# Log-sum-exp over rows: moving the early logarithm forward and redrawing the table of chunks

## Chip, cores, metric

One core of a Trainium2 chip. The metric is the device time of the kernel in microseconds (us), as a median of several executions. The profile is one execution; its "span" runs from the first to the last instruction and is some 1.8 us shorter than the time. All runs quoted here are on record as undisturbed ("fast"), with a granted clock of 1.0. TensorE does nothing in this kernel. "DVE" is VectorE, "ACT" is ScalarE, "SPq" is the queue of SyncE, which issues the loads.

## The reference

```python
x = np.random.randn(32, 512, 1024).astype(np.float32)   # 64 MiB (67.1 MB)
x_max = np.max(x, axis=-1, keepdims=True)
out = x_max.squeeze(-1) + np.log(np.sum(np.exp(x - x_max), axis=-1))
```

With normal inputs the kernels take log(sum(exp(x))) without the maximum, and both pass the comparison with the reference.

## The kernel before

The 16,384 rows lie as 128 rows on each of 128 partitions. "A row" below means one such row on all 128 partitions: 128 x 1024 numbers, 512 KB. The rows are loaded in 18 chunks into a ring of 51 row slots. A pair `(rows, n_dve)` in the table says how many rows a chunk has and how many of them take the first of two ways:

- *bulk rows*: one Exp of ScalarE over all `n_dve` rows, then one sum of VectorE;
- *accumulator rows*: one Exp of ScalarE per row, which sums along the row as it goes; a short accumulator read follows.

```python
CHUNKS = [
    (4, 0), (16, 10), (14, 13), (15, 4), (16, 7), (15, 6), (12, 9), (9, 6), (7, 5), (5, 4),
    (4, 3), (3, 3), (2, 2), (2, 0), (1, 1), (1, 0), (1, 0), (1, 0),
]
RING_ROWS = 51
LN_EARLY = 6
# ... cut: tensors, semaphores, place[i] = (ring slot, first row) ...
    def take_logs(lo, hi, dve_wait, act_wait):
        nonlocal acts
        nc.scalar.wait_ge(act_done, act_wait)
        nc.scalar.wait_ge(dve_done, dve_wait)
        nc.scalar.activation(out=res[:, lo:hi], in_=sums[:, lo:hi], func=Ln).then_inc(
            act_done, 1
        )
        acts += 1
# ... cut ...
    for i, (r, n_dve) in enumerate(CHUNKS):
        if i:
            load(i)              # SyncE waits until the ring slots are free, then issues
        s, row = place[i]
        if i == len(CHUNKS) - LN_EARLY:
            logged = place[i - 1][1]
            take_logs(0, logged, *done_before[i - 1])
        nc.scalar.wait_ge(landed[i], 16)
        if n_dve:
            nc.scalar.activation(
                out=ring[:, s : s + n_dve], in_=ring[:, s : s + n_dve], func=Exp
            ).then_inc(act_done, 1)
            acts += 1
            nc.vector.wait_ge(act_done, acts)
            nc.vector.reduce_sum(
                out=sums[:, row : row + n_dve], in_=ring[:, s : s + n_dve], axis=AX
            ).then_inc(dve_done, 1)
            # ... cut ...
        for j in range(n_dve, r):
            nc.scalar.activation(
                out=ring[:, s + j],
                in_=ring[:, s + j],
                func=Exp,
                accum_out=sums[:, row + j : row + j + 1],
            ).then_inc(act_done, 1)
            # ... cut ...
    take_logs(logged, NB, dves, acts)
    nc.scalar.wait_ge(act_done, acts)
    nc.scalar.dma_start(out=out_v, in_=res).then_inc(stored, 16)
```

So one Ln over the first 117 columns of sums stands before chunk 12, and the other 11 columns are done at the end.

Of the kernel before, what the change touches and what calls it, by code (L numbers as in the profile page):

```python
# [1 line left out]

# [4 lines left out]



CHUNKS = [  # L10
    (4, 0), (16, 10), (14, 13), (15, 4), (16, 7), (15, 6), (12, 9), (9, 6), (7, 5), (5, 4),
    (4, 3), (3, 3), (2, 2), (2, 0), (1, 1), (1, 0), (1, 0), (1, 0),
]
RING_ROWS = 51

LN_EARLY = 6


@with_exitstack
def kernel(  # L20
    ctx: ExitStack,
    tc: tile.TileContext,
    x: bass.AP,
    axis: bass.AP,
    out: bass.AP,
):
    nc = tc.nc
    P = nc.NUM_PARTITIONS

    assert axis in (-1, len(x.shape) - 1), f"only last-axis reduction supported, got {axis}"  # L30

    x_flat = x.flatten_outer_dims()
    N, D = x_flat.shape
    assert N % P == 0
    NB = N // P
    assert sum(r for r, _ in CHUNKS) == NB

    fp32 = mybir.dt.float32
    Exp = mybir.ActivationFunctionType.Exp
    Ln = mybir.ActivationFunctionType.Ln  # L40
    AX = mybir.AxisListType.X

    x_v = x_flat.rearrange("(p t) d -> p t d", p=P)
    out_v = bass.AP(tensor=out.tensor, offset=out.offset, ap=[[NB, P], [1, NB]])

    ring = nc.alloc_sbuf_tensor("ring", [P, RING_ROWS, D], fp32).ap()
    sums = nc.alloc_sbuf_tensor("sums", [P, NB], fp32).ap()
    res = nc.alloc_sbuf_tensor("res", [P, NB], fp32).ap()

    landed = [tc.alloc_semaphore(f"landed{i}") for i in range(len(CHUNKS))]  # L50
    act_done = tc.alloc_semaphore("act_done")
    dve_done = tc.alloc_semaphore("dve_done")
    stored = tc.alloc_semaphore("stored")


    hook = nc.pop_inst_callback()
    symbolic, nc._always_lower_symbolic_ap = nc._always_lower_symbolic_ap, False


    place = []  # L60
    row = slot = 0
    for r, _ in CHUNKS:
        if slot + r > RING_ROWS:
            slot = 0
        place.append((slot, row))
        slot += r
        row += r



    busy = [(0, 0)] * RING_ROWS
    acts = dves = 0

    def load(i):
        (s, row), r = place[i], CHUNKS[i][0]
        act_wait = max(a for a, _ in busy[s : s + r])
        dve_wait = max(d for _, d in busy[s : s + r])
        if dve_wait:
            nc.sync.wait_ge(dve_done, dve_wait)
        if act_wait:  # L80
            nc.sync.wait_ge(act_done, act_wait)
        nc.sync.dma_start(out=ring[:, s : s + r], in_=x_v[:, row : row + r]).then_inc(  # L82
            landed[i], 16
        )

    def take_logs(lo, hi, dve_wait, act_wait):
        nonlocal acts
# [7 lines that stand above are left out]
    body = nc.main_func.blocks[-1]  # L95
    assert not body.instructions
    load(0)
    n_early = len(body.instructions)

    nc.scalar.preload_act_table_set("natural_log_exp_and_others")  # L100

    logged = 0
    done_before = [(0, 0)]
    for i, (r, n_dve) in enumerate(CHUNKS):
        if i:
            load(i)
        s, row = place[i]
        if i == len(CHUNKS) - LN_EARLY:
            logged = place[i - 1][1]
            take_logs(0, logged, *done_before[i - 1])  # L110
        nc.scalar.wait_ge(landed[i], 16)
        if n_dve:
            nc.scalar.activation(  # L113
                out=ring[:, s : s + n_dve], in_=ring[:, s : s + n_dve], func=Exp
# [6 lines that stand above are left out]
            dves += 1  # L121
            for j in range(n_dve):
                busy[s + j] = (0, dves)
# [8 lines that stand above are left out]
            busy[s + j] = (acts, 0)  # L132
        done_before.append((dves, acts))
# [4 lines that stand above are left out]
    nc.gpsimd.wait_ge(stored, 16)  # L138



    sp = mybir.EngineType.SP
    first = nc.main_func.blocks[0]
    head, work = first.instructions, body.instructions
    at = next(k for k, i in enumerate(head) if i.engine == sp and i.opcode == "Drain")
    end = next(k for k, i in enumerate(head) if i.opcode == "UnconditionalBranch")
    first.instructions = head[:at] + work[:n_early] + head[at:end] + work[n_early:] + head[end:]
    body.instructions = []

    nc._always_lower_symbolic_ap = symbolic  # L150
    nc.push_inst_callback(hook)


# [1 line left out]
_INS = ['x', 'axis']  # L155
_OUTS = [((32, 512), 'float32')]

_NUMBERS = {'axis': -1}


# [26 lines left out]
```

## Time and profile before

| | before |
|---|---|
| time, median of the first 3 runs | 164.24 us (164.04 to 164.56) |
| span of the profiled run | 162.7 us |
| load queue, busy share of 16 DMA engines | 96.1% |
| ScalarE / VectorE busy | 76% / 49% |
| final Ln starts | 159.94 us |

The page's queue line of the kernel before: packets, MB moved, share of the span of all 16 DMA engines.

```profile
q1 hardware_dynamic: 2592, 67.11, 96.1%
```

96.1% of 162.7 us is 156.3 us: the loads fill the program but for its first microsecond and its end. As long as the packets take as long as they do here, nothing that only rearranges work on the engines can go below that.

The waits view of the same profile: engine, line, operand, what it waited for; total us, number of waits, the longest.

```profile
DVE sums L118 <- ACT ring L113: 79.0, 5, 35.6
ACT ring L113 <- DMA ring<-in_x_dram: 30.2, 5, 15.0
ACT ring L125 <- DMA ring<-in_x_dram: 5.5, 1, 5.5
...
ACT res L90 <- DVE sums L118: 0.4, 1, 0.4
```

ScalarE waits for loads six times, the last time before chunk 5 at 99.85 us. After that its only recorded wait is 0.4 us before the early Ln (L90), for VectorE's sums.

The timeline of its end: start, duration, engine, line, operation. L125 is an accumulator row, L90 the Ln.

```profile
151.67 0.30 ACT L90 ACTIVATE res<-sums 128x117 f32<-128x117 f32 x1 [0.41 <-DVE sums L118]
...
157.74 1.04 ACT L125 ACTIVATE ring<-ring 128x1024 f32<-128x1024 f32 x1
...
158.78 1.04 ACT L125 ACTIVATE ring<-ring 128x1024 f32<-128x1024 f32 x1
159.72 0.18 ACT L125 ACTIVATION_READ_ACCUMULATOR ring<-ring 128x1 f32 x1
159.94 0.21 ACT L90 ACTIVATE res<-sums 128x11 f32<-128x11 f32 x1
```

### The profile page before, as it was taken

What the parts mean: (1) busy time and instruction counts of PE and PEld (TensorE: products, weight loads), DVE (VectorE), ACT (ScalarE), POOL (GpSimd) and SP (SyncE); (2) the same over time, 40 slices, a digit from 0 to 9 for tenths busy, and PEclk for the clock granted to TensorE, in tenths of its full rate; (3) what the DMA queues carried; (4) which work ended last, traced back from release to release, by engine and by line L of the source; (5) the groups of instructions that cost most, each with busy time, mean ns of one, the idle gap of its engine ahead of it and who ended that gap; (6) DMA issues with size and microseconds to landing.
All of it is one profiled execution on the core that took longest, in us unless ns stands there. A gap on an engine that the chain in (4) does not pass through costs nothing.

```text
span 162.7 us, 208 instructions
## 1 busy us (share of the span) xinstructions
DVE 79.2 (49%) x13; ACT 123.2 (76%) x126; POOL 0.2 (0%) x4
## 2 busy tenths in 40 slices
DVE  0000000029940499990003940194009999999980
ACT  3180004999599707999099984999999999999893
POOL 0000000000000000000000000000000000000000
DMA  7997999989999979989997998998999999999960
GB/s 262 511 515 306 467 515 437 409 352 409 439 483 483 468 321 451 515 354 421 499 468 332 408 483 387 435 507 362 426 435 415 430 423 432 420 420 422 405 268 16
DMA packets 2737, 67.18 MB, mean 413 GB/s; under 512 B 304, under 2 KB 432, under 8 KB 944
## 3 DMA queue, kind: packets, MB, share of 16 engines
q1 hardware_dynamic: 2592, 67.11, 96.1%
q10 hardware_dynamic: 144, 0.07, 0.1%
q14 instruction: 1, 0.01, 0.0%
HBM read 67.11 MB, written 0.07 MB: 413 GB/s over the span
## 4 chain that ended last, share of the span: by engine, by line
DMA 45%; DVE 27%; ACT 26%; issue 0%; SPq 0%; ACTq 0%
DMA ring<-in_x_dram 45%; DVE sums L118 27%; ACT ring L113 17%; ACT ring L125 9%; ACT res L90 0%; SPq L82 0%; ACTq L89 0%
## 5 line engine op out<-in xcount | busy, mean ns | idle before, releaser
L118 DVE TENSOR_REDUCE sums<-ring 128x4 f32<-128x4096 f32 (+9 forms) x13 | 79.2, 6138 | 79.0 <-ACT ring L113 79.0
L113 ACT ACTIVATE ring<-ring 128x4096 f32<-128x4096 f32 (+9 forms) x13 | 64.8, 4987 | 30.3 <-DMA ring<-in_x_dram 30.2
L125 ACT ACTIVATE ring<-ring 128x1024 f32<-128x1024 f32 x55 | 57.2, 1040 | 5.5 <-DMA ring<-in_x_dram 5.5
L125 ACT ACTIVATION_READ_ACCUMULATOR ring<-ring 128x1 f32 x55 | 10.3, 187 | 0.0
L100 ACT ACT_TABLE_LOAD x1 | 1.3, 1283 | 0.8 <-PEq L168 0.8
L90 ACT ACTIVATE res<-sums 128x117 f32<-128x117 f32 (+1 forms) x2 | 0.5, 256 | 0.4 <-DVE sums L118 0.4
L168 POOL MEMSET const-bfloat16-1.0<- 128x1 bf16 x1 | 0.1, 102 | 0.0
L168 POOL MEMSET const-uint8-127<- 128x1 uint8 x1 | 0.1, 102 | 0.0
L168 POOL MEMSET const-float32-0.0<- 128x1 f32 x1 | 0.1, 99 | 0.2 <-issue 0.2
L168 POOL MEMSET const-float32-1.0<- 128x1 f32 x1 | 0.1, 99 | 0.0
## 6 DMA issues: line engine op xcount, KB each, us to landing
ring<-in_x_dram SPq DMA_DIRECT2D x2, 7680.0 KB, 45.3
ring<-in_x_dram SPq DMA_DIRECT2D x1, 7168.0 KB, 42.6
ring<-in_x_dram SPq DMA_DIRECT2D x1, 6144.0 KB, 40.9
ring<-in_x_dram SPq DMA_DIRECT2D x1, 4608.0 KB, 29.7
ring<-in_x_dram SPq DMA_DIRECT2D x2, 2048.0 KB, 20.0
ring<-in_x_dram SPq DMA_DIRECT2D x1, 3584.0 KB, 36.5
ring<-in_x_dram SPq DMA_DIRECT2D x1, 2560.0 KB, 28.1
ring<-in_x_dram SPq DMA_DIRECT2D x2, 1024.0 KB, 29.4
```

Source lines behind the costliest of these rows:

```text
L90: nc.scalar.activation(out=res[:, lo:hi], in_=sums[:, lo:hi], func=Ln).then_inc(act_done, 1)
L100: nc.scalar.preload_act_table_set("natural_log_exp_and_others")
L113: nc.scalar.activation(out=ring[:, s : s + n_dve], in_=ring[:, s : s + n_dve], func=Exp).then_inc(act_done, 1)
L118: nc.vector.reduce_sum(out=sums[:, row : row + n_dve], in_=ring[:, s : s + n_dve], axis=AX).then_inc(dve_done, 1)
L125: nc.scalar.activation(out=ring[:, s + j], in_=ring[:, s + j], func=Exp, accum_out=sums[:, row + j : row + j + 1],).then_inc(act_done, 1)
L168: nc = _bacc.Bacc("TRN2", target_bir_lowering=False, num_devices=1)
```

## The change

Its intent: keep the early Ln from interrupting ScalarE near the end, by putting it in front of chunk 5, and draw the chunks so that the shares of ScalarE and VectorE fit the moments at which the chunks land. The new list for the first load, FIRST_PARTS, is set to one load as before; the placement code at the end was made general. Neither is meant to change what runs.

```diff
 CHUNKS = [
-    (4, 0), (16, 10), (14, 13), (15, 4), (16, 7), (15, 6), (12, 9), (9, 6), (7, 5), (5, 4),
-    (4, 3), (3, 3), (2, 2), (2, 0), (1, 1), (1, 0), (1, 0), (1, 0),
+    (4, 1), (15, 11), (16, 10), (16, 15), (16, 0), (14, 0), (12, 9), (9, 5), (7, 5), (5, 4),
+    (4, 3), (3, 0), (2, 2), (2, 2), (1, 0), (1, 0), (1, 0),
 ]
-LN_EARLY = 6
+LN_AT = 5
+FIRST_PARTS = [("sync", 0, 128)]
@@ in the loop over chunks
-        if i == len(CHUNKS) - LN_EARLY:
-            logged = place[i - 1][1]
-            take_logs(0, logged, *done_before[i - 1])
-        nc.scalar.wait_ge(landed[i], 16)
+        if i == LN_AT:
+            logged = row
+            take_logs(0, logged, *done_before[i])
+        nc.scalar.wait_ge(landed[i], 16 * (len(FIRST_PARTS) if i == 0 else 1))
```

(Cut: the loop over FIRST_PARTS in `load`, and the placement of the first load.)

More of the change, by code (lines that the diff above doesn't have):

```diff
@@ L81, in load @@
             nc.sync.wait_ge(act_done, act_wait)
-        nc.sync.dma_start(out=ring[:, s : s + r], in_=x_v[:, row : row + r]).then_inc(
-            landed[i], 16
-        )
+        for engine, lo, hi in FIRST_PARTS if i == 0 else [("sync", 0, P)]:
+            getattr(nc, engine).dma_start(
+                out=ring[lo:hi, s : s + r], in_=x_v[lo:hi, row : row + r]
+            ).then_inc(landed[i], 16)
     def take_logs(lo, hi, dve_wait, act_wait):
@@ L138 @@
     nc.gpsimd.wait_ge(stored, 16)
-    sp = mybir.EngineType.SP
     first = nc.main_func.blocks[0]
     head, work = first.instructions, body.instructions
-    at = next(k for k, i in enumerate(head) if i.engine == sp and i.opcode == "Drain")
     end = next(k for k, i in enumerate(head) if i.opcode == "UnconditionalBranch")
-    first.instructions = head[:at] + work[:n_early] + head[at:end] + work[n_early:] + head[end:]
+    head, tail = head[:end], head[end:]
+    for ins in work[:n_early]:
+        at = next(
+            k for k, i in enumerate(head) if i.engine == ins.engine and i.opcode == "Drain"
+        )
+        head.insert(at, ins)
+    first.instructions = head + work[n_early:] + tail
     body.instructions = []
```

## The prediction

> **What bounds the kernel now.** The loads. The queue table gives the load queue 96.1% of 16 engines' span (156.3 of 162.7 us). By windows of one microsecond, data flows from 1.2 until about 157.3 us, with no lasting hole: 67.11 MB / 156.1 us = 430 GB/s. The Trainium skill ("DMA: Bandwidth & Descriptors", Specifications) puts the fabric ceiling at 435 GB/s; the trace is about 1% below, so reordering chunks can hardly shorten this part.
>
> Then comes a tail. In the timeline ScalarE is busy from 99.85 us (landing of row 80) to 159.9, except 0.41 us before the first Ln, where it waits for VectorE's sums (waits view). The final Ln starts at 159.94, the span ends at 162.7. The last row lands at about 157.5 at the latest and costs 1.04 us plus an accumulator read, so the final Ln could start at about 158.7 at best. What can be removed is 1.2 us, 0.7%. The 45% DMA of the chain of waits understates the loads: the chain follows the backlogged engines.
>
> **What the change does**, with the trace's durations (bulk Exp 0.107 + 0.853 us per row as pitch, row with accumulator 1.04, VectorE sum 0.13 + 1.07 per row, rows landing every 1.21 us):
> - The early Ln leaves the saturated stretch: 0.41 wait + 0.30 work. It moves to about 101 us, the edge of ScalarE's last idle gap. Exp and Ln share a table set (Trainium skill, "ScalarE: Activation LUTs", Table sets; the trace has one table load of 1.28 us), so moving it adds no load.
> - ScalarE's work after chunk 5 lands: before, 39 bulk rows in 9 instructions plus 24 accumulator rows = 59.2 us from 99.85. After, 30 bulk rows in 7 plus 31 accumulator rows = 58.6 us, but chunk 5 ends one row later, landing at about 101.0. Chunk 4 (16 accumulator rows, 16.6 us from about 84.1) ends at 100.8, then Ln until about 101.0. The last Exp ends at about 159.7.
> - VectorE ends its last sum at 159.3 to 159.5 instead of 158.2: nearly a tie with ScalarE.
> - The final Ln takes 61 columns instead of 11: +0.04 us.
> - One load fewer: 128 of 2592 packets. In a stream without holes, nothing visible.
> - The first four chunks fill the ring exactly (51 rows). Chunk 4's load can issue at about 47 us (VectorE done with chunk 1) while queued data last until 64; chunk 7's at about 94 with data until 115. No hole.
> - The rewritten placement leaves the first load where it was.
>
> **Sum:** on the critical path 0.7 us leaves with Ln and 0.6 us of work, 1.15 us of later landing comes in: the final Ln moves by about -0.2 us (estimate, +-0.6). Predicted 164.0 us, 163.3 to 164.7. Chances: faster by over 2% 0.01, within 2% 0.98, slower 0.01.
>
> **What the profile would show.** Right: load queue again about 156 us busy, data ending at 157 to 158; Ln at about 101 with little wait before it; ScalarE unbroken from 101 to about 159.6; last VectorE sum within 1 us of the last Exp; final Ln at 159.2 to 160.2. Wrong: a hole in the load stream after 20 us, an idle gap of ScalarE over 0.5 us after 101, or Ln waiting for VectorE.
>
> **What would make it wrong.** A load queue that runs dry at a ring wait, since chunks 4 and 5 keep all rows on ScalarE; a stream whose rate changes by 1% with chunk sizes (1.6 us, more than all the rest); or VectorE, with two 2-row sums at the end, finishing over 1 us after ScalarE.

## The result, and the profile after

The changed kernel took 164.12 us (median of 6 runs, 163.90 to 164.65), the kernel before 164.28 us (6 runs). The ratio of the fast runs is 0.9994, with a 95% interval of 0.9974 to 1.0015. Ratios here are the mean time of one kernel's fast runs over that of the other's in the same rounds, so they are not quite the ratio of the medians. In a second comparison (run `a_again` below) the ratio was 0.9982 (0.9965 to 0.9999). The change is worth at most about 0.3%, and the first comparison alone does not tell it from nothing; the 0.2 us predicted lie in both intervals.

The page's queue line of the changed kernel, and its waits view:

```profile
q1 hardware_dynamic: 2448, 67.11, 96.4%
```

```profile
DVE sums L121 <- ACT ring L116: 85.9, 7, 29.6
ACT ring L116 <- DMA ring<-in_x_dram: 29.4, 4, 14.0
ACT ring L128 <- DMA ring<-in_x_dram: 5.3, 1, 5.3
...
```

96.4% of 162.2 us is again 156.4 us of loading. The wait of the Ln for VectorE is gone. The timeline of the changed kernel, at the new place of the Ln and at the end:

```profile
99.29 1.04 ACT L128 ACTIVATE ring<-ring 128x1024 f32<-128x1024 f32 x1
...
100.46 0.26 ACT L93 ACTIVATE res<-sums 128x67 f32<-128x67 f32 x1
100.67 1.06 ACT L128 ACTIVATE ring<-ring 128x1024 f32<-128x1024 f32 x1
...
157.15 1.04 ACT L128 ACTIVATE ring<-ring 128x1024 f32<-128x1024 f32 x1
...
158.19 1.04 ACT L128 ACTIVATE ring<-ring 128x1024 f32<-128x1024 f32 x1
159.14 0.19 ACT L128 ACTIVATION_READ_ACCUMULATOR ring<-ring 128x1 f32 x1
159.36 0.25 ACT L93 ACTIVATE res<-sums 128x61 f32<-128x61 f32 x1
```

The final Ln starts 0.58 us earlier than in the profile before, 159.36 instead of 159.94. The medians moved by only 0.16 us. The six times of the changed kernel range over 0.75 us, and its profiled execution (163.96 us) is one of its faster ones, while that of before (164.53 us) is one of its slower ones. **One pair of profiles exaggerates the difference here**; 0.43 us of the 0.58 us is another course of the load stream and not the change, as the table under b_half and a_again shows.

### The profile page after: what moved, and what is told of

Same layout as the page of the kernel before. It is cut to its first block, busy times and chain, and to the rows that moved or that the text cites. A ratio compares the mean times of both kernels' runs of the same rounds, so it can differ in the third digit from the quotient of the medians.

```text
span 162.2 us, 213 instructions
## 1 busy us (share of the span) xinstructions
DVE 72.9 (45%) x11; ACT 124.1 (76%) x136; POOL 0.2 (0%) x4
## 3 DMA queue, kind: packets, MB, share of 16 engines
q1 hardware_dynamic: 2448, 67.11, 96.4%
HBM read 67.11 MB, written 0.07 MB: 414 GB/s over the span
## 4 chain that ended last, share of the span: by engine, by line
ACT 52%; DMA 38%; DVE 7%; issue 1%
DMA ring<-in_x_dram 38%; ACT ring L128 30%; ACT ring L116 22%; DVE sums L121 7%; ACT res L93 0%
## 5 line engine op out<-in xcount | busy, mean ns | idle before, releaser
L121 DVE TENSOR_REDUCE sums<-ring 128x5 f32<-128x5120 f32 (+8 forms) x11 | 72.9, 6648 | 86.0 <-ACT ring L116 85.9
L116 ACT ACTIVATE ring<-ring 128x5120 f32<-128x5120 f32 (+8 forms) x11 | 59.3, 5394 | 29.4 <-DMA ring<-in_x_dram 29.4
L128 ACT ACTIVATE ring<-ring 128x1024 f32<-128x1024 f32 x61 | 63.4, 1041 | 5.3 <-DMA ring<-in_x_dram 5.3
L128 ACT ACTIVATION_READ_ACCUMULATOR ring<-ring 128x1 f32 x61 | 11.4, 187 | 0.0
L93 ACT ACTIVATE res<-sums 128x67 f32<-128x67 f32 (+1 forms) x2 | 0.5, 256 | 0.1
```

The lines of the kernel that those rows point to most:

```text
L116: nc.scalar.activation(out=ring[:, s : s + n_dve], in_=ring[:, s : s + n_dve], func=Exp).then_inc(act_done, 1)
L121: nc.vector.reduce_sum(out=sums[:, row : row + n_dve], in_=ring[:, s : s + n_dve], axis=AX).then_inc(dve_done, 1)
L128: nc.scalar.activation(out=ring[:, s + j], in_=ring[:, s + j], func=Exp, accum_out=sums[:, row + j : row + j + 1],).then_inc(act_done, 1)
```

## The experiments

Ten kernels ran. I name the theories: A, the early Ln cost its wait and its work in ScalarE's unbroken stretch; B, the new chunk table brings the gain; C, the load stream alone sets the time; and D, formed after eight runs. The first four shared one set of rounds (before: 164.50 us), the next four another (before: 164.46 us), and the last two a third (before: 164.76 us).

### b_ln5: the old table with only the Ln moved

```diff
-        if i == len(CHUNKS) - LN_EARLY:
-            logged = place[i - 1][1]
-            take_logs(0, logged, *done_before[i - 1])
+        if i == 5:
+            logged = row
+            take_logs(0, logged, *done_before[i])
```

> The kernel before with its own chunk table, only the early Ln moved to the start of chunk 5. Theory A (the Ln was the cost: its 0.41 us wait and 0.30 us of work stood in ScalarE's unbroken stretch): the Ln falls into the idle gap of ScalarE before chunk 5 (97.1 to 99.85 us in the profile of before), the final Ln starts 0.6 to 0.8 us earlier, near 159.2, and the time falls by 0.5 to 0.8 us, to 163.5 to 163.8: as much as, or more than, the whole change. Theory B (the new chunk table brings the gain, the Ln's place is nothing): final Ln stays at 159.8 to 160.1, time 164.2. Theory C (the load stream alone sets the time): no change beyond 0.1 us.

Measured: 164.26 us (ratio 0.9985, 0.9973 to 0.9998), 0.24 us below before by medians. The sign is that of theory A; the size is a third to a half of it. (Theory B's 164.2 us is met as a number, but before took 164.50 us in these rounds, and the final Ln at 159.67 us lies outside B's range.) The timeline shows where the rest went: L125 is an accumulator row, L90 the Ln.

```profile
97.19 0.26 ACT L90 ACTIVATE res<-sums 128x65 f32<-128x65 f32 x1
99.77 5.32 ACT L113 ACTIVATE ring<-ring 128x6144 f32<-128x6144 f32 x1 [2.32 <-DMA ring<-in_x_dram]
...
153.39 1.06 ACT L125 ACTIVATE ring<-ring 128x1024 f32<-128x1024 f32 x1 [0.40 <-DMA ring<-in_x_dram]
...
159.67 0.26 ACT L90 ACTIVATE res<-sums 128x63 f32<-128x63 f32 x1
```

The Ln now runs inside an idle gap, where it delays nothing. But at 153.39 us ScalarE waits 0.40 us for a load, a wait that before did not have. So most of the 0.71 us taken away came back, and the final Ln moved by 0.27 us. ScalarE had not been behind the loads by as much as its unbroken stretch suggested.

### b_noln: the old table with no early Ln at all

```diff
-        if i == len(CHUNKS) - LN_EARLY:
-            logged = place[i - 1][1]
-            take_logs(0, logged, *done_before[i - 1])
```

> The kernel before with no early Ln at all: one Ln over all 128 columns at the end. Theory A: the wait and the work leave the stretch, the final Ln grows by 117 columns x 0.833 ns = 0.10 us; it starts near 159.2, ends about 0.6 us earlier than before; time 163.5 to 163.8, the same as with the Ln at chunk 5 within 0.15 us. Then an early Ln was never worth having. Rival: the early Ln hides real work, so without it the time is at best that of before, 164.2 or more.

Measured: 164.37 us (ratio 0.9995, 0.9981 to 1.0009), outside theory A's 163.5 to 163.8; the rival's "164.2 or more" is met. It waits the same 0.40 us at 153.35 us and starts the final Ln at 159.63 us. That Ln takes 0.31 us over 128 columns, against 0.21 us over 11 in the kernel before. So splitting off an early Ln saves at most 0.1 us of the end; the rounds can't tell whether even that is felt.

### a_lnback and a_noln: the new table with the Ln back, and with none

```diff
 a_lnback
-        if i == LN_AT:
-            logged = row
-            take_logs(0, logged, *done_before[i])
+        if i == len(CHUNKS) - 6:
+            logged = place[i - 1][1]
+            take_logs(0, logged, *done_before[i - 1])
 a_noln: these three lines taken out
```

> The changed kernel with its new chunk table, only the early Ln put back six chunks short of the end. Theory A: the Ln's work of about 0.26 us returns to ScalarE's unbroken stretch; VectorE is done with chunk 9 at about 148, so there is no wait this time; final Ln about 159.6 instead of 159.36, time up 0.2 to 0.3 us from the changed kernel, 164.3 to 164.4. Theory B: no loss, 164.1.

> The changed kernel with no early Ln at all. Theory A: the Ln at chunk 5 was almost fully hidden (0.1 us of idle before it, and chunk 5 had not landed), so taking it out gains at most 0.1 us and the longer final Ln costs 0.06 us: time equal to the changed kernel within 0.15 us, 164.0 to 164.2. Rival (the early Ln at chunk 5 is what brings the gain by shortening the last Ln): slower than the changed kernel by 0.3 us or more.

Measured: 164.30 us with the Ln back (ratio 0.9989, 0.9976 to 1.0001), and 164.36 us with none (0.9991, 0.9979 to 1.0004). Both are in the range of the changed kernel and of each other; the changed kernel itself did not run in these rounds. a_lnback shows an Ln of 0.28 us with no wait:

```profile
149.75 0.28 ACT L93 ACTIVATE res<-sums 128x114 f32<-128x114 f32 x1
...
158.73 1.04 ACT L128 ACTIVATE ring<-ring 128x1024 f32<-128x1024 f32 x1
...
159.90 0.21 ACT L93 ACTIVATE res<-sums 128x14 f32<-128x14 f32 x1
```

Its raw times alone do not separate the theories: the second chunk's Exp starts at 26.08 us there and at 25.76 in a_noln, and the final Ln starts 0.21 us later, 159.90 against 159.69. Counted from the landing of the last load they do (the table under b_half and a_again). a_noln asks whether the changed kernel needed an early Ln at all: within the resolution of these rounds, it did not.

The times of the four runs do not place the change's gain: either part alone stays within 0.25 us of before, and no combination is clear of the others.

### a_half: the engines taken out of the way

The Exps and sums work on the first 512 of each row's 1024 columns, the loads are whole. Its output is wrong, which doesn't matter for the time.

```diff
-                out=ring[:, s : s + n_dve], in_=ring[:, s : s + n_dve], func=Exp
+                out=ring[:, s : s + n_dve, : D // 2],
+                in_=ring[:, s : s + n_dve, : D // 2],
+                func=Exp,
 (the same for the sums of VectorE and for the accumulator rows)
```

> Wrong on purpose: the changed kernel, with ScalarE and VectorE working on the first 512 of each row's 1024 columns; the loads are the same. It measures the load stream with engines that never lag. Theory A (loads end at about 157.3 us and the engines add a lag of about 1 us at the end): load data again until 157 to 157.5 us, the final Ln starts at about 158.1 to 158.3, and the time falls by 1.0 to 1.4 us from the changed kernel, to 162.7 to 163.1. Rival (engines bound the kernel, as an unbroken ScalarE suggests): loads get faster or the time falls by several us.

Measured: 163.87 us (ratio 0.9964, 0.9949 to 0.9979). That is 0.39 us below the faithful a_extra_early of the same rounds (164.26 us), where 1.0 to 1.4 was expected. With half the work ScalarE waits for every load at the end, so its timeline shows the landings themselves. L130 is an accumulator row, L93 the Ln:

```profile
156.07 0.63 ACT L130 ACTIVATE ring<-ring 128x512 f32<-128x512 f32 x1 [0.23 <-DMA ring<-in_x_dram]
...
157.35 0.63 ACT L130 ACTIVATE ring<-ring 128x512 f32<-128x512 f32 x1 [0.55 <-DMA ring<-in_x_dram]
...
158.57 0.63 ACT L130 ACTIVATE ring<-ring 128x512 f32<-128x512 f32 x1 [0.50 <-DMA ring<-in_x_dram]
...
159.32 0.25 ACT L93 ACTIVATE res<-sums 128x61 f32<-128x61 f32 x1
```

**The last row is usable at 158.57 us, not at 157.5 as I had predicted.** Why I had read it wrongly shows in the end of the load stream, in windows of 0.2 us of the same profile. Columns: window, length, busy time of DVE, ACT and POOL, granted clock, mean busy share of the 16 DMA engines, GB/s.

```profile
156.80:157.00 0.20, 0.20 (x1) 0.00 (x0) 0.00 (x0) 1.00 0.78 307
157.00:157.20 0.20, 0.10 (x1) 0.00 (x0) 0.00 (x0) 1.00 0.43 164
157.20:157.40 0.20, 0.00 (x0) 0.05 (x1) 0.00 (x0) 1.00 0.51 205
157.40:157.60 0.20, 0.00 (x0) 0.20 (x1) 0.00 (x0) 1.00 0.26 102
157.60:157.80 0.20, 0.00 (x0) 0.20 (x1) 0.00 (x0) 1.00 0.06 21
157.80:158.00 0.20, 0.00 (x0) 0.20 (x2) 0.00 (x0) 1.00 0.10 41
158.00:158.20 0.20, 0.00 (x0) 0.07 (x1) 0.00 (x0) 1.00 0.00 0
```

The 16 engines don't end together: the share fades for about a microsecond, from 0.78 before 157.0 us to nothing after 158.0. (The view books a packet in the window in which it starts; the last one starts before 158.0 us and, by its record in the trace, ends at 158.12.) The trace dates 16 increments of each load's semaphore, and ScalarE waits for all 16. For the last load here they run from 157.45 to 158.55 us, and ScalarE starts 0.02 us after the last one. The profile of the kernel before had this too: 157.40 to 158.51 us, so my 157.5 lies near the first increment and a microsecond before the last. From the last data to the 16th increment 0.43 us pass (0.41 to 0.45 in all twelve profiles). The Trainium skill gives a reason in "DMA: Bandwidth & Descriptors", section "Anatomy of one DMA": the semaphore is updated only after the last byte is confirmed as landed, and most of the fixed cost of a DMA (about 2 us there, fitted on another way of issuing) is this receipt. The trace agrees that such a delay exists, with 0.43 us after the last data; that the receipt is its cause no run here shows.

From the landing at 158.57 us, a full row would need 512 columns more of Exp, at the 0.853 us of a 1024-column row in the bulk instructions 0.43 us more. Its final Ln could then start at 159.32 + 0.43 = 159.75 us at the best. The faithful kernels start theirs at 159.36 (the changed one), 159.61 (a_extra_early) and 159.65 us (a_again). Streams differ by some tenths between executions, so single profiles can't say more. The times say that the 0.39 us of a_half is about what the shorter last row gives by itself; a reserve of the changed kernel beyond that can't be seen.

### a_extra_early and a_extra_late: the same extra work in two places

```diff
+    scratch = nc.alloc_sbuf_tensor("scratch", [P, D // 2], fp32).ap()
+        if i == 3:                    # a_extra_late: i == 9
+            for k in range(3):
+                nc.scalar.wait_ge(extra, 1 + k)
+                nc.scalar.activation(out=scratch, in_=scratch, func=Exp).then_inc(extra, 1)
```

(Cut: the semaphore `extra` and one clearing of the tile by GpSimd, which sets it to 1.)

> The changed kernel with three extra 512-column Exps on a scratch tile (about 0.61 us each, 1.8 to 2.2 us with their waits) on ScalarE before chunk 3, where it idles 4.4 us. Theory A: free, time within 0.1 us of the changed kernel, 164.0 to 164.2. Rival (ScalarE's total busy time counts): slower by about 2 us.

> The same three extra Exps before chunk 9, inside ScalarE's unbroken stretch. Theory A: passes one for one, the final Ln 1.6 to 2.2 us later, time 165.7 to 166.3. Theory C (the load stream alone sets the time): less than 0.5 us slower.

Measured: early 164.26 us (ratio 0.9989), late 166.23 us (ratio 1.0109, 1.0094 to 1.0124). The extra group from the timelines of the two, first a_extra_early, then a_extra_late:

```profile
60.03 1.94 ACT L121 ACTIVATE scratch<-scratch 128x512 f32<-128x512 f32 x3
64.59 13.00 ACT L124 ACTIVATE ring<-ring 128x15360 f32<-128x15360 f32 x1 [2.62 <-DMA ring<-in_x_dram]
```

```profile
141.66 1.94 ACT L121 ACTIVATE scratch<-scratch 128x512 f32<-128x512 f32 x3
143.50 3.60 ACT L124 ACTIVATE ring<-ring 128x4096 f32<-128x4096 f32 x1
```

1.94 us of work before chunk 3 shortened a wait for the load, which still is 2.62 us, and cost nothing that these rounds can see. The same before chunk 9 cost 1.97 us. That rules out theory C for work *added* late: ScalarE has no reserve there. Together with b_ln5 it gives an asymmetry. ScalarE keeps pace with the landings almost exactly, so late work added to the new table costs all of itself, and late work removed returns only what ScalarE lagged, about a quarter of a microsecond in the old table.

### a_rowloads: what the number of loads costs

```diff
-        for engine, lo, hi in FIRST_PARTS if i == 0 else [("sync", 0, P)]:
-            getattr(nc, engine).dma_start(
-                out=ring[lo:hi, s : s + r], in_=x_v[lo:hi, row : row + r]
-            ).then_inc(landed[i], 16)
+        for j in range(r):
+            nc.sync.dma_start(
+                out=ring[:, s + j], in_=x_v[:, row + j]
+            ).then_inc(landed[i], 16)
-        nc.scalar.wait_ge(landed[i], 16 * (len(FIRST_PARTS) if i == 0 else 1))
+        nc.scalar.wait_ge(landed[i], 16 * r)
```

> The changed kernel with every chunk loaded row by row: 128 loads of 512 KB in place of 17, about 18,400 packets instead of 2448; ring and engines unchanged. It measures what number and size of the loads cost. Theory A (packets of 4 KB flow at 406 GB/s against about 430, as the last windows show): stream 9 us longer at most, time 168 to 173. If so, 17 instead of 18 loads is worth under 0.1 us. Rival (loads overlap fully, number doesn't matter): within 1 us of the changed kernel.

Measured: 172.63 us (ratio 1.0499, 1.0484 to 1.0515), within the 168 to 173 us expected. The page's queue line:

```profile
q1 hardware_dynamic: 18432, 67.12, 98.8%
```

The final Ln moved to 168.00 us, and the stream ran at about 410 GB/s through the page's slices, against 430 before. The packets rose by 18,432 - 2448 = 15,984, 999 for each of 16 engines, and the time by 172.63 - 164.26 = 8.37 us (against a_extra_early, which has the changed kernel's loads). So a packet more costs an engine about 8.4 ns. This is an estimate: the number of loads, of packets and their size changed together. (SyncE issues for 152 us there, but the engines are busy for 98.8% of the span, so I take the packets as the cause.) The changed kernel has 144 packets fewer than before, 9 an engine, worth 0.08 us by this slope (an estimate from these two runs). The Trainium skill ("DMA: Bandwidth & Descriptors", Rules for kernel authors) asks for 128 partitions and at least 1 MiB a DMA for the most bandwidth; these half-MiB loads of 4 KB pieces agree, at a loss of 5% of the stream's rate.

### b_half and a_again: is the last landing the same for both tables?

b_half is the cut of a_half made in the kernel before. a_again is the changed kernel, unaltered.

> Wrong on purpose: the kernel before, with ScalarE and VectorE on half of each row's columns, so that the landing of every load of the old chunk table shows. Theory D (formed after the first eight runs: both chunk tables land the last row at the same time, about 158.3 to 158.6 us, about 1.2 us after the mean engine's data end; before lagged behind it by only 0.2 to 0.3 us): final Ln at 159.1 to 159.5, time about 0.6 us below before, ratio 0.995 to 0.998, as the same cut of the changed kernel gave (0.9964). Rival (17 loads in place of 18 make the changed kernel's stream shorter): the last row lands 0.3 us or more later than in the cut of the changed kernel, ratio to before above 0.998.

> The changed kernel unaltered, for a comparison in the same rounds. Theory D: it is at the landing's pace already, so the cut of the engines' work gains only the half of the last row's Exp, about 0.43 us: 0.3 to 0.6 us above the halved kernel, 0.05 to 0.3 us below before (ratio 0.998 to 0.9997). Rival (the changed kernel leads by what its profile showed, 0.58 us earlier final Ln): ratio 0.9965.

Measured: b_half 163.96 us (ratio to before 0.9957, 0.9940 to 0.9973; 0.80 us below it by medians where 0.6 was expected), a_again 164.43 us (0.9982, 0.9965 to 0.9999). The end of b_half's timeline (L127 an accumulator row, L90 the Ln):

```profile
158.79 0.63 ACT L127 ACTIVATE ring<-ring 128x512 f32<-128x512 f32 x1 [0.50 <-DMA ring<-in_x_dram]
...
159.55 0.21 ACT L90 ACTIVATE res<-sums 128x11 f32<-128x11 f32 x1
```

The last row landed at 158.79 us here, 0.22 us later than in a_half and 0.2 us outside what D expected (landing up to 158.6; the final Ln, expected up to 159.5, is 0.05 us outside). The ratios say more than two single profiles: the cut makes the kernel before 0.43% faster and the changed one 0.36%, intervals overlapping. The rival, which wanted a ratio above 0.998 for b_half, falls. The chunk table did not shorten the stream in a way these rounds can see. a_again is 0.33 us below before by medians and 0.47 us above b_half, both about as D had it (the first 0.03 us more than expected). The 0.47 us is near the 0.43 us of the half row; the rounds show no further reserve on the changed kernel's engines.

The semaphore's increments settle what the times can't. For each profile: the 16th increment of the last load, the start of the last row's Exp (both in us), and ScalarE's lag, which is the difference.

| profile | early Ln | last load landed | last Exp starts | lag |
|---|---|---|---|---|
| before | before chunk 12 | 158.51 | 158.78 | 0.27 |
| b_ln5 | before chunk 5 | 158.43 | 158.51 | 0.07 |
| b_noln | none | 158.41 | 158.47 | 0.06 |
| b_half | before chunk 12 | 158.77 | 158.79 | 0.02 |
| after | before chunk 5 | 158.08 | 158.19 | 0.11 |
| a_again | before chunk 5 | 158.35 | 158.48 | 0.13 |
| a_extra_early | before chunk 5 | 158.31 | 158.45 | 0.14 |
| a_extra_late | before chunk 5 | 158.60 | 160.52 | 1.92 |
| a_lnback | before chunk 11 | 158.46 | 158.73 | 0.27 |
| a_noln | none | 158.40 | 158.53 | 0.13 |
| a_half | before chunk 5 | 158.55 | 158.57 | 0.02 |

(One execution each; b_half and a_half do half the work.) With all the work done and none added late, the lag is 0.27 us where the Ln stands late and 0.06 to 0.14 us where it does not, in either table: taking the Ln out of the stretch is worth 0.13 to 0.2 us, and the new table adds nothing to it that shows here. In before the Ln puts ScalarE 0.92 us behind at chunk 12 (b_ln5: 0.21), but 0.23 us at chunk 13 (b_ln5: 0.02, after a wait), so most of it is lost in a gap that would have been there. The landing itself differs by as much between profiles of one kernel (after and a_again: 0.27 us) as between the tables.

No tried version that gives right results beats the changed kernel clearly: ratios to before are 0.9985 (b_ln5), 0.9989 (a_lnback and a_extra_early), 0.9991 (a_noln), 0.9995 (b_noln), and 0.9994 and 0.9982 for the changed kernel itself.

## Why the prediction was right, and where it was not

- **The time.** Predicted 164.0 us (163.3 to 164.7), measured 164.12; "within 2%" held.
- **The loads bound the kernel; reordering can't shorten them.** Right: 156.3 us of queue time before, 156.4 after, no hole at a ring wait. The 430 GB/s stay just below the 435 GB/s quoted from the skill.
- **The marks named for the profile.** All came: Ln at 100.46 us without a wait, ScalarE without a wait in the view to 159.23 us, the last sum of VectorE within a microsecond of it, the final Ln in the stated range. But VectorE ended at 158.87 us and not at 159.3 to 159.5: the near tie with ScalarE did not come.
- **ScalarE's work after chunk 5.** Predicted 58.6 us; from 100.67 to the final Ln at 159.36 it is 58.7 us. The agreement doesn't show that this work is the critical path: at chunks 6, 7 and 13 ScalarE starts 0.02 us after the landing, so there the loads set its pace.
- **The step that failed: "The last row lands at about 157.5 at the latest", hence "What can be removed is 1.2 us".** In the profile of before itself the last load landed at 158.51 us, and with the engines out of the way (a_half, b_half) the last row is usable at 158.57 and 158.79 us. I had read the end of data as the moment at which the *mean* of the 16 engines' busy share fell off, and had left out the stragglers and the delay from last data to the waiting engine. What could be removed was ScalarE's lag of 0.27 us, of which b_ln5 removed 0.2 us.
- **The mis-sized term: 0.7 us for the Ln.** The work and the wait were there as read, 0.30 and 0.41 us. But removing them alone moved the final Ln by 0.27 us, about 0.2 of lag and 0.08 of an earlier landing, since the rest turned into a wait for a load. On the other side stood "1.15 us of later landing" and 0.6 us less work on ScalarE; the profile pair shows chunk 5 starting 0.82 us later (100.67 against 99.85). Neither reaches the end, because ScalarE waits for later loads again. The sum took ScalarE for one chain from chunk 5 to the end, and that path was wrong. Terms too large with opposite signs left a small sum. That the total agrees confirms the loads' bound; for my split of the last 0.7 us it is luck.
- **A slip:** the change removes 144 packets, not 128; each load also has 16 small ones (4 bytes each).

What stays open is what separates executions of one kernel by up to 0.75 us, more than the whole effect; the spans show that it is in the run itself, and the profiles that landings shift by some tenths (the Exp of the second chunk of the changed kernel's table starts at 25.62 to 26.08 us).

## What to carry to other kernels

An engine that is busy without a break is not yet the limit: halve its work with the loads unchanged, and see whether it starts to wait for every load. If it kept pace, removing its late work returns only its lag, while adding late work costs in full. When a load stream is the bound, date a load's end by the last increment of its semaphore or by an instruction that waited for it, not by where the mean share of the DMA engines drops, and take differences below half a percent from several rounds and never from one pair of profiles.

## What the Trainium skill lacked or had wrong

- "DMA: Bandwidth & Descriptors" tells of the receipt after the last byte and says that the engines finish independently, but not how far apart they end a saturated stream: in a_half the 16 increments of the last load spread over 1.1 us, in the changed kernel over 0.6 us, and the last came 0.43 to 0.45 us after the last data.
- The same page's section "Where 436 GB/s comes from" says that for transfers between HBM and SBUF a limit of about 358 GB/s per core binds. For one core alone it does not: the page's own largest measurement is 425 GB/s, and here one core read 67.11 MB in about 156.1 us, 430 GB/s.
- The same page has a time per packet for one small transfer, but none for a full stream of loads: about 8.4 ns per packet and engine by a_rowloads (an estimate).
- "ScalarE: Activation LUTs" has no figure for an Exp that also gives its accumulator: here it costs 1.04 us per 1024-column row from start to start, with a read of 0.19 us that mostly overlaps, against 0.853 us for a row within a large Exp.
